# Two-layer S5 and attention trunk: GELU as one ScalarE function, rotation tables kept on chip, tables in buffers of their own, a new order

## The chip, the cores and the metric

One core of one Trainium2 chip runs the whole program. The metric is the device time of one execution in microseconds (us); lower is better. Engines are named as in the profile: PE (TensorE matmul), PEld (its weight loads), DVE (VectorE), ACT (ScalarE), POOL (GpSimd), SP (SyncE, which issues most DMAs).

## The reference

Two layers over 512 tokens of width 1024. Each has an S5 state-space group (32 groups of 16 channels, 64 complex states) and four heads of differential attention on the same modulated input, one output projection, and a SwiGLU channel mixer. Cut to the part that the change touches:

```python
for l in range(DEPTH):                       # 2
    h = x * (1.0 + scale1) + shift1
    u, q, k, v = split(h @ w_in[l])
    # S5: x_t = Lb * x_(t-1) + Bb u_t, complex and diagonal; Lb = exp((a_re + i a_im) * delta)
    y = Re(C x) + d_skip * u
    y = jax.nn.gelu(y)                       # the tanh form: 0.5 y (1 + tanh(sqrt(2/pi) (y + 0.044715 y^3)))
    y = y * sigmoid(y @ glu_w + glu_b)
    att = diff_attention(rot(q), rot(k), v)  # two softmax maps per head, causal
    x = layer_norm(ALPHA * x + (1 + gate1) * (concat(y, att) @ w_out))
    x = layer_norm(ALPHA * x + (1 + gate2) * swiglu(x * (1 + scale2) + shift2))
```

## The kernel before, in words

Every matrix product is made of three single-pass products (high by high, high by low, low by high; `mm3`, L118). A weight tile `wraw` comes by DMA, ACT makes its high part `whi` (`cp`, L113) and DVE, or POOL for a few, the low part `wlo` (L104).

**Layer 0 starts** with a loop over the eight 128-row slices of the input (`START`, L20): for each slice DVE makes two modulation columns (`mraw`, L110), ACT and DVE the two parts of `hT`, PE the products `ups`. In the same loop the S5 parameters are worked out by the generator `s5_params` in five parts; `OPT["par"]` says for each part whether DVE or POOL does it (before: POOL for all but part 2, which holds only ACT's sines). POOL also makes the position angles `rang` there.

**S5 works on four quarters q**, eight groups each. `s5_build` makes the tables of a quarter on DVE (`G`, `QT`, with a temporary `ta`), the short convolution kernel `ksb` that is written to the DRAM array `kd` by DMA and read back by eight DMAs as `M`, and the transposed `Q` (PE `qps`, ACT). `s5_rot` makes cosine and sine of the rotation (`cs`, and `ns` for the negated sine) with ACT's Sin, writes them to the DRAM array `sC` with two DMAs and `s5_gen` reads them back as `csl`. `s5_scan` multiplies (`vps` on PE, then DVE `rp`, `wz`), scans, rotates back and adds the halves with two instructions into the states `S`. `s5_out` makes `yps` on PE and the GELU: ACT Square, a DVE step, ACT Tanh, a second DVE step (both `gl`), ACT Copy into the layout of `y`.

**Two rings of buffers matter.** All S5 work on PE (`kps`, `qps`, `utp`, `vps`, `yps`, `ytps`) shares one PSUM bank (tag "s5", `PB`). The temporaries `ta`, `btmp`, `thl`, `dt`, `ksb`, `cs`, `ns` and `gl` share two buffers (tag "t5", `TB`).

**The order** of the mixer is written in ticks: each short piece of the main products is a tick, and `PLAN[l]` lists for each kind ("s5", "att", "bld", "cs", "mod", "pf") the ticks at which its next step is issued; a scheduler then orders each engine. Layer 1 has the same steps, its tables are built during layer 0's channel mixer and kept in DRAM (`kd`, `sG`, `sQ`, `sC`).

Of the kernel before, what the change touches and what calls it, by code (L numbers as in the profile page):

```python
# [13 lines left out]
AF = mybir.ActivationFunctionType  # L14
# [5 lines left out]
START = ['', '', '', 'v', 'ppvV', 'rpV', 'ApvvA', 'VAVVb']  # L20
LAG, LAG1 = 2, 1
PLAN = ({'bld': [1.264, 2.8128, 2.8128, 7.5302, 15.0069, 15.7908, 16.6324, 22.2347, 24.025, 24.025, 24.025, 31.5693, 31.8037, 32.6247, 36.6694, 39.8654, 39.8664, 44.4181, 55.2875, 55.2875], 's5': [2.4963, 13.7411167, 15.82, 17.6903, 17.9768, 17.9768, 28.1555, 32.3101, 33.8664, 33.8664, 41.8348, 41.8348, 41.8348, 44.9401, 56.3771, 61.9808, 63.9276, 74.4357, 74.4357, 74.9633], 'att': [32.6299, 32.6299, 32.6299, 34.4688, 34.4688, 37.9126, 37.9126, 37.9126, 38.4369, 42.2702, 48.2563, 48.2563, 48.2563, 48.2563, 53.3008, 55.2114, 55.2114, 55.2114, 62.4974, 64.6963, 65.1666, 65.1666, 66.8965, 69.8788, 69.8788, 69.8788, 69.8788, 69.8788, 72.9166, 73.1266492, 78.0578164, 79.4594, 84.4816, 84.4816, 84.4816, 84.4816, 84.4816, 85.7045, 86.611, 86.611, 86.611, 87.1372, 87.1372, 87.1372, 87.1372, 87.1372, 87.1372, 87.1372, 87.1372, 87.1372, 87.7613, 88.3711, 92.1141, 94.0138, 95.5657, 99.9], 'mod': [10.9986, 18.0979, 25.5229, 28.8809, 38.8480964, 39.702, 45.7126, 48.3167, 48.3167, 49.5891, 50.7771, 51.8893, 59.3159, 62.6235, 62.6235, 62.6235, 65.1638, 68.4286, 78.3464, 89.495], 'pf': [15.904, 15.9839, 26.2995, 26.2995, 39.217, 46.2033, 61.5805, 61.9828, 61.9828, 77.3237, 84.6088, 88.9481, 89.2859, 89.9011], 'cs': [2.3738, 2.3738, 3.9308, 15.3106]}, {'s5': [0, 9.5668, 14.1521, 22.5905, 23.0853, 23.0853, 28.7962, 33.7987, 53.4804, 53.9093, 54.6366, 54.6366, 54.6366, 54.89, 57.9461, 62.766, 63.1181, 64.2437, 76.6993, 79.0981], 'att': [32.001, 32.001001, 32.001001, 32.001001, 32.001001, 36.2691, 36.9654, 49.5504, 49.5634, 49.946, 52.2004, 52.2014, 52.2014, 53.123, 53.4199, 53.4634231, 53.4644231, 54.3593, 56.3216, 58.3250688, 61.5574297, 61.5584297, 62.6277, 62.6277, 64.4714996, 64.4715006, 64.4715016, 64.4715026, 64.4715036, 64.4715046, 64.4715056, 64.4715066, 64.4715076, 64.4715086, 64.4715096, 64.4715106, 64.4715116, 64.4715126, 82.7565, 82.7565, 82.7566, 82.7566, 83.9079, 87.4356, 87.4366, 87.4376, 90.018, 91.9921, 91.9931, 91.9941, 91.9951, 91.9951, 91.9951, 91.9951, 91.9951, 99.9], 'pf': [1.9638689, 9.1450603, 14.6524633, 14.6534633, 19.9457, 32.098, 37.9847, 48.098, 51.1731991, 74.7986995, 74.7986995, 81.1276, 84.5849, 86.8909]})
OPT = {'par': [0, 0, 1, 0, 0], 'MODQ': 'sync', 'q_bld': 1, 'q_s5': 0, 'q_att': 0, 'q_pf': 0, 'CSQ': 'scalar', 'plo': [[1, 0, 1, 0, 0, 0, 0, 0, 0, 0, 0, 1, 0, 0, 0, 0, 0, 0], [0, 0, 0, 0, 0, 0, 0, 1, 1, 0, 0, 0, 0, 1, 0, 0, 0, 0]]}
# [3 lines left out]
P = 128  # L27
# [28 lines left out]
T1, T2 = _split_const(2.0 * math.pi, (17,))  # L56
PI_LO = float(np.nextafter(np.float32(math.pi), np.float32(0)))
GELU_C = float(np.float32(math.sqrt(0.044715)))
GELU_S = float(np.float32(math.sqrt(2.0 / math.pi)))
FREQS = [float(np.float32(THETA) ** np.float32(-(2 * i) / ROT)) for i in range(ROT // 2)]  # L60


# [1324 lines left out]
```

## Time and profile before

| | |
|---|---|
| median of 3 runs | 1258.78 us (1256.43 to 1260.86) |
| the profiled execution's own time | 1254.48 us |
| its span, first to last instruction | 1252.7 us |
| mean granted clock of TensorE | 0.985 |
| busy: PE, DVE, ACT, POOL | 1186.2, 813.6, 481.9, 162.3 us |

The span has seven stages: the start of layer 0 (0 to 62 us), its mixer (62 to 286), its channel mixer (286 to 640), the change of layers (640 to 670), and for layer 1 mixer (670 to 881), channel mixer (881 to 1240) and end. A busy time of PE counts a matmul's whole stay in the array, so that a full PE shows 100%. "L107" is a line of the kernel, often that of a helper, so that groups are told apart by tile names.

### The profile page before, as it was taken

Reading aid. Unit: us, or ns where it says so; the run is one execution under the profiler, and the core shown is the slowest. Engines: PE = TensorE matmul, PEld = TensorE weight load, DVE = VectorE, ACT = ScalarE, POOL = GpSimd, SP = SyncE. Lnnn points to the kernel's source line nnn. Section 1 sums busy time; section 2 is a strip of 40 time slices with the busy share of each in tenths; the row PEclk is TensorE's granted clock in tenths of the full one; section 3 lists DMA queues with packets and bytes.
Section 4 is the critical chain, followed back from the end, with each engine's and each line's share of the span. In section 5 each row is a group of like instructions: output and inputs, shape, how many; then the busy total and the mean of one; then the engine's idle time right before and its main releaser. Section 6 shows DMA issues by size and latency. Waiting matters only on the chain.

```text
span 1252.7 us, 17629 instructions
## 1 busy us (share of the span) xinstructions
PE 1186.2 (95%) x6736; PEld 988.7 (79%) x6736; DVE 813.6 (65%) x1505; ACT 481.9 (38%) x848; POOL 162.3 (13%) x289
## 2 busy tenths in 40 slices
PE   4898788999999999999999999999999999999997
PEld 3687676779888888888877788877988888888885
DVE  6779798786787675798558366757665222244556
ACT  3436255536222222343446355553623222234330
POOL 8921230010000010000001243000000000000001
PEclk9899789999999999999999999999999999999999
DMA  9784535535577577645334663223463333333241
GB/s 351 270 209 125 105 84 167 176 128 166 187 256 270 178 234 192 199 157 166 102 98 144 195 178 102 72 97 102 158 192 97 93 100 101 97 89 117 68 134 68
DMA packets 60469, 188.68 MB, mean 151 GB/s; under 512 B 8065, under 2 KB 13985, under 8 KB 60385
## 3 DMA queue, kind: packets, MB, share of 16 engines
q1 hardware_dynamic: 51408, 170.94, 43.0%
q0 software_dynamic: 5088, 13.42, 4.1%
q10 hardware_dynamic: 3888, 3.20, 1.0%
q8 instruction: 53, 0.87, 0.3%
q14 instruction: 32, 0.25, 0.1%
HBM read 172.90 MB, written 12.53 MB: 148 GB/s over the span
## 4 chain that ended last, share of the span: by engine, by line
PE 73%; DVE 11%; POOL 6%; DMA 4%; issue 4%; ACT 2%; DVEq 0%; POOLq 0%; ACTq 0%
PE gps L116 39%; PE dps L116 18%; PE ops L116 4%; PE qkps L116 2%; PE vps L116 2%; POOL s5tmp L104 1%; PE ups L116 1%; DVE wlo L104 1%; DMA wraw<-in_wst 1%; PE glups L116 1%; PE po L116 1%; DVE mraw L110 1%; DVE x L107 1%; PE sps L757 1%; DMA kd<-ksb 1%
## 5 line engine op out<-in xcount | busy, mean ns | idle before, releaser
L104 DVE TENSOR_TENSOR wlo<-wraw,whi 128x1024 fp32r<-128x1024 f32 x180 | 219.6, 1222 | 262.8 <-ACT whi L113 262.1
L113 ACT ACTIVATE whi<-wraw 128x1024 fp32r<-128x1024 f32 x184 | 194.2, 1057 | 390.3 <-PE gps L116 249.8
L116 PE MATMUL gps<-hT2h,whi 128*128 128x512 f32 (+1 forms) x768 | 286.5, 373 | 0.6 <-DVE rtmp L104 0.4
L116 PE MATMUL gps<-hT2l,whi 128*128 128x512 f32 (+1 forms) x768 | 285.8, 372 | 0.0
L116 PE MATMUL gps<-hT2h,wlo 128*128 128x512 f32 (+1 forms) x768 | 285.4, 372 | 0.0
L116 PE MATMUL dps<-whi,ah 128*128 128x512 f32 x704 | 219.6, 391 | 0.0
L116 PEld LDWEIGHTS gps<-hT2h,whi 128*128 128x128 f32 x768 | 144.7, 188 | 26.0 <-DVE rtmp L104 0.9
L116 PEld LDWEIGHTS gps<-hT2l,whi 128*128 128x128 f32 x768 | 144.7, 188 | 24.9
L116 PEld LDWEIGHTS gps<-hT2h,wlo 128*128 128x128 f32 x768 | 144.7, 188 | 24.9
L116 PEld LDWEIGHTS dps<-whi,ah 128*128 128x128 f32 x704 | 132.2, 188 | 28.6 <-DVE rtmp L104 1.2
L116 PE MATMUL dps<-wlo,ah 128*128 128x512 f32 x352 | 137.1, 390 | 0.0
L110 DVE SCALAR_TENSOR_TENSOR mraw<-mraw,scb 128x1024 f32<-128x1024 f32 x96 | 114.2, 1219 | 5.4 <-DMA mraw<-in_modw 5.4
L113 ACT ACTIVATE ah<-aT 128x512 fp32r<-128x512 f32 x88 | 53.6, 626 | 91.2 <-PE dps L116 72.8
L104 DVE TENSOR_TENSOR ah<-aT,ah 128x512 fp32r<-128x512 f32 x88 | 59.3, 688 | 41.3 <-ACT ah L113 41.1
L116 PEld LDWEIGHTS dps<-wlo,ah 128*128 128x128 f32 x352 | 66.1, 188 | 13.4
L116 PE MATMUL ops<-whi,am 128*128 128x512 f32 x128 | 43.1, 398 | 0.0
L761 ACT ACTIVATE e<-sps,nm 128x128 f32<-128x128 f32 (+3 forms) x64 | 33.3, 525 | 19.3 <-DVE nm L759 18.7
L554 POOL DMA_DIRECT2D M<-kd x64 | 33.8, 535 | 41.0 <-DMA kd<-ksb 37.9
L116 PE MATMUL qkps<-wlo,hTh 128*128 128x256 f32 x128 | 38.1, 298 | 0.5 <-DVE wlo L104 0.5
L116 PE MATMUL qkps<-whi,hTh 128*128 128x256 f32 x128 | 37.9, 298 | 0.0
L116 PE MATMUL qkps<-whi,hTl 128*128 128x256 f32 x128 | 37.9, 297 | 0.0
L116 PE MATMUL qkps<-whi,hTnh 128*128 128x256 f32 x128 | 37.4, 293 | 0.0
(285 smaller groups left out, 1858.9 us busy)
## 6 DMA issues: line engine op xcount, KB each, us to landing
wraw<-in_wst SPq DMA_DIRECT2D x184, 512.0 KB, 3.7
mraw<-in_modw SPq DMA_DIRECT2D x96, 512.0 KB, 5.1
M<-kd POOLq DMA_DIRECT2D x64, 64.0 KB, 4.4
gb<-in_lnr SPq DMA_DIRECT2D x8, 512.0 KB, 3.9
csl<-sC SPq DMA_DIRECT2D x8, 384.0 KB, 3.7
xT<-in_xT SPq DMA_DIRECT2D x8, 256.0 KB, 6.7
x<-in_x SPq DMA_DIRECT2D x4, 512.0 KB, 4.6
G<-gd SPq DMA_DIRECT2D x4, 512.0 KB, 4.8
```

The costliest lines, as they stand in the source:

```text
L104: (eng or nc.vector).tensor_tensor(out, a, b, op=op)
L107: nc.vector.scalar_tensor_tensor(out, a, s, b, op0=op0, op1=op1)
L110: nc.vector.scalar_tensor_tensor(out, a, s, b, op0=ALU.mult, op1=ALU.mult, accum_out=acc_out)
L113: nc.scalar.activation(out, in_, AF.Copy, scale=scale)
L116: nc.tensor.matmul(ps, a, b, start=start, stop=stop)
L554: nc.gpsimd.dma_start(M[16 * j : 16 * j + 16], ksrc)
L757: nc.tensor.matmul(ps[:, m, c_], qT[rows, i * P : (i + 1) * P], kT[rows, c_], start=False, stop=c_.stop == n)
L761: nc.scalar.activation(e[:, m, :n], ps[:, m, :n], AF.Exp, bias=nm[:, m : m + 1], accum_out=ss[:, i, m : m + 1])
```

## The change

The GELU of `s5_out` becomes one ACT function that reads PSUM and writes `y`'s layout. In layer 0 `s5_rot` leaves its table in SBUF (`tri`, one buffer of its own) instead of writing it to `sC` and reading it back; it runs for quarter q+1 behind the scan of quarter q. Layer 1 writes its table with one DMA instead of two. `ksb` gets a buffer of its own. The two adds of the states become one instruction. `START`, `PLAN` and `OPT` are new: parts 1 and 3 of the parameters go to DVE, builds are no longer held behind the engine's newest instruction (`q_bld`). Rows of `PLAN` are left out.

```diff
-START = ['', '', '', 'v', 'ppvV', 'rpV', 'ApvvA', 'VAVVb']
+START = ['', 'v', '', 'p', 'vpr', 'VVp', 'vpvA', 'AVbVVA']
...
-OPT = {'par': [0, 0, 1, 0, 0], 'MODQ': 'sync', 'q_bld': 1, 'q_s5': 0, 'q_att': 0, 'q_pf': 0, 'CSQ': 'scalar', 'plo': [[1, 0, 1, 0, 0, 0, 0, 0, 0, 0, 0, 1, 0, 0, 0, 0, 0, 0], [0, 0, 0, 0, 0, 0, 0, 1, 1, 0, 0, 0, 0, 1, 0, 0, 0, 0]]}
+OPT = {'par': [0, 1, 0, 1, 0], 'MODQ': 'sync', 'q_bld': 0, 'q_s5': 0, 'q_att': 0, 'q_pf': 0, 'CSQ': 'scalar', 'plo': [[1, 0, 1, 0, 0, 0, 0, 0, 0, 0, 0, 1, 0, 0, 0, 0, 0, 0], [0, 0, 0, 0, 0, 0, 0, 1, 1, 0, 0, 0, 0, 1, 0, 0, 0, 0]]}
...
-            ksb = t5([P, P], name="ksb")
+            ksb = sm([P, P], "ksb", 1)
...
-            cs = t5([P, 2, 4, 64], name="cs")
+
+            tri = sm([P, 768], "tri", 1)
+            cs = tri[:, 256:].rearrange("p (r g k) -> p r g k", r=2, g=4)
...
-            ns = t5([P, 256], name="ns")
-            ts(ns, flat(st), -1.0, ALU.mult)
-            eng = getattr(nc, "gpsimd" if l else OPT["CSQ"])
-            eng.dma_start(sC[q][:, 256:768], cs.rearrange("p r g k -> p (r g k)"))
-            eng.dma_start(sC[q][:, 0:256], ns)
+            ts(tri[:, 0:256], flat(st), -1.0, ALU.mult)
+            if l:
+                nc.gpsimd.dma_start(sC[q], tri)
+            return tri
...
-            for o in range(2):
-                po, pj = (pr[:, o, j].rearrange("p (g k) -> p g k", g=4)[:, :, 0:63] for j in range(2))
-                tt(S[:, o, :, 1:64], po, pj, ALU.add)
+            po, pj = (pr[:, :, j].rearrange("p o (g k) -> p o g k", g=4)[:, :, :, 0:63] for j in range(2))
+            tt(S[:, :, :, 1:64], po, pj, ALU.add)
...
-            gl = t5([P, 512], name="gl")
-            nc.scalar.activation(gl, ps, AF.Square, scale=GELU_C)
-            stt(gl, gl, 1.0, ps, ALU.add, ALU.mult)
-            nc.scalar.activation(gl, gl, AF.Tanh, scale=GELU_S)
-            stt(gl, gl, 1.0, ps, ALU.add, ALU.mult)
-            cp(yo, gl.rearrange("p (a i c) -> p a i c", a=4, i=8), scale=0.5)
+            nc.scalar.activation(yo, ps.rearrange("p (a i c) -> p a i c", a=4, i=8), AF.Gelu_apprx_tanh)
...
-                C[q] = sm([P, 768], "csl", 1)
-                nc.sync.dma_start(C[q], sC[q])
+                if l:
+                    C[q] = sm([P, 768], "tri", 1)
+                    nc.sync.dma_start(C[q], sC[q])
+
+            def rot(q):
+                C[q] = s5_rot(0, q, pms[0])
...
+            if l == 0:
+
+                seq = [(rot, (0,))] + [(fn, (q + (fn is rot),)) for q in range(4) for fn in (inp, inT, scan, rot, sout)
+                                       if fn is not rot or q < 3]
```

Three places of the new order. **DVE in layer 0's builds**, before: the kernel table `ksb` of quarter 2 and the half `QT` behind it (`ta` is the temporary, `mraw` a modulation column, `gl` the GELU).

```order
L107 SCALAR_TENSOR_TENSOR ksb<-mask_86,s5dt,ksb 128x16
L104 TENSOR_TENSOR QT<-pw,s5bc 128x512
L104 TENSOR_TENSOR ta<-pw,s5bc 128x512
L104 TENSOR_TENSOR QT<-pw,s5bc 128x512
L104 TENSOR_TENSOR QT<-QT,ta 128x512
L104 TENSOR_TENSOR ta<-pw,s5bc 128x512
L110 SCALAR_TENSOR_TENSOR mraw,mods<-mraw,scb 128x1024
L104 TENSOR_TENSOR QT<-QT,ta 128x512
L107 SCALAR_TENSOR_TENSOR gl<-gl,yps 128x512
```
The same engine in the change, at the end of the builds; `rho`, `e`, `nm` are the attention's.

```order
L105 SCALAR_TENSOR_TENSOR e<-e,rho 128x384
L443 COPY s5bc<-s5bc 64x8x16 x2
L102 TENSOR_TENSOR ta<-pw,s5bc 128x512
L102 TENSOR_TENSOR Gt<-pw,s5bc 128x4x128
L102 TENSOR_TENSOR Gt<-Gt,ta 128x4x128
L102 TENSOR_TENSOR ta<-pw,s5bc 128x512
L758 TENSOR_REDUCE nm<-sps 128x2
L102 TENSOR_TENSOR Gt<-Gt,ta 128x4x128
L102 TENSOR_TENSOR QT<-pw,s5bc 128x512 x2
L763 RECIPROCAL rho<-ss 128x1
L105 SCALAR_TENSOR_TENSOR ksb<-mask_86,s5dt,ksb 128x16
```
The builds' `Gt`, `QT` and `ta` now stand among attention steps instead of behind `ksb`, and no `gl` row is left.

**ACT in layer 0's mixer**, before: the GELU of quarter 0 among the attention's work (`e` is the exponential, `wT` the transposed map).

```order
L113 ACTIVATE UU<-u_129 128x512
L634 ACTIVATE gl<-yps 128x512
L113 ACTIVATE wT<-sps 128x384
L636 ACTIVATE gl<-gl 128x512
L785 ACTIVATE e,q_1226<-po 128x128
L113 ACTIVATE wT<-sps 128x512
L113 ACTIVATE y<-gl 128x4x8x16
L113 ACTIVATE UU<-utp 128x512
L785 ACTIVATE e,q_1226<-po 128x128
```
In the change, the GELU of quarter 1 (L629), the rotation's sine and cosine of quarter 2 (`tri`, L224) and the exponentials (L760).

```order
L629 ACT_TABLE_LOAD
L629 ACTIVATE y<-yps 128x4x8x16
L760 ACT_TABLE_LOAD
L760 ACTIVATE e,ss<-sps,nm 128x128 x2
L111 ACTIVATE UU<-utp 128x512
L760 ACTIVATE e,ss<-sps,nm 128x256
L224 ACT_TABLE_LOAD
L224 ACTIVATE tri<-thl 128x256
L225 ACTIVATE tri<-thl 128x256
L111 ACTIVATE wT<-sps 128x128
L760 ACT_TABLE_LOAD
L760 ACTIVATE e,ss<-sps,nm 128x256
```
Three ACT passes have become one, and the three functions bring a table load each time they alternate. Over the whole program the change has 23 table loads where the kernel before has 8: 11 against 3 in layer 0's mixer, 8 against 1 in layer 1's, 4 elsewhere in both.

**POOL in layer 0's mixer**, before: the reads of `M`, and the decay table `dt` and first state `wz` that a scan needs.

```order
L104 TENSOR_TENSOR es<-es,mhalf 128x4
L610 MEMSET wz 128x8
L554 DMA M<-kd_123 16x8x128 x8
L583 COPY dt<-r_396 128x256
L584 MEMSET dt 128x4
L554 DMA M<-kd_123 16x8x128 x2
L610 MEMSET wz 128x8
L554 DMA M<-kd_123 16x8x128 x6
L583 COPY dt<-r_396 128x256
L584 MEMSET dt 128x4
L610 MEMSET wz 128x8
```
The same in the change, for quarters 2 and 3.

```order
L552 DMA M<-kd_123 16x8x128 x8
L581 COPY dt<-r_402 128x256
L102 TENSOR_TENSOR es<-es,mhalf 128x4
L552 DMA M<-kd_123 16x8x128
L582 MEMSET dt 128x4
L552 DMA M<-kd_123 16x8x128
L608 MEMSET wz 128x8
L552 DMA M<-kd_123 16x8x128 x6
L581 COPY dt<-r_402 128x256
```
The second half of the `dt` of quarter 2 now stands behind one read of quarter 3's `M`, which waits for that quarter's `ksb` in DRAM; before it stood ahead. On PE the counts tell the shift: of layer 0's 384 `qkps` matmuls 77 stand behind the last S5 `vps`, before 28, and on DVE 7 of the 16 attention score tiles have had their maximum (`nm`) taken by the last scan's second rotation, before 9.

## Rows read from the trace of the kernel before

**Rows 1.** page: busy us by engine; clock in 40 slices, tenths

```profile
PE 1186.2 (95%) x6736; PEld 988.7 (79%) x6736; DVE 813.6 (65%) x1505; ACT 481.9 (38%) x848; POOL 162.3 (13%) x289
PEclk9899789999999999999999999999999999999999
```

**Rows 2.** windows by stage: PE, PEld, DVE, ACT, POOL busy (count), clock, DMA, GB/s

```profile
0.00:62.00 62.00, 38.63 (x138) 30.13 (x139) 41.57 (x74) 25.60 (x36) 54.89 (x99) 0.92 0.87 311
62.00:205.00 143.00, 119.53 (x1135) 104.75 (x1134) 122.80 (x276) 64.87 (x145) 33.13 (x62) 0.93 0.54 139
205.00:286.00 81.00, 78.12 (x393) 60.79 (x391) 65.56 (x136) 39.06 (x90) 7.39 (x9) 0.98 0.46 146
286.00:640.00 354.00, 353.87 (x1782) 295.72 (x1782) 251.78 (x466) 119.21 (x171) 18.49 (x33) 1.00 0.59 190
670.00:881.00 211.00, 205.02 (x1472) 172.08 (x1471) 135.42 (x271) 103.35 (x230) 39.55 (x72) 1.00 0.41 125
881.00:1240.00 359.00, 358.73 (x1674) 300.40 (x1675) 164.58 (x220) 112.07 (x150) 4.16 (x7) 1.00 0.36 110
```

**Rows 3.** waits of DVE, 60 to 290 us: total us, times, longest us

```profile
DVE ta L104 <- DMA kd<-ksb: 7.1, 1, 7.1
DVE btmp L104 <- POOL pw L104: 4.0, 1, 4.0
DVE thl L104 <- DMA sC<-ns: 1.0, 1, 1.0
```

**Rows 4.** waits of PE, 60 to 290 us

```profile
PE qps L495 <- DVE gl L107: 4.5, 1, 4.5
PE ytps L643 <- DVE gl L107: 1.1, 1, 1.1
```

**Rows 5.** tile gl, 60 to 260 us: ns min/median/max, first, last start

```profile
L107 DVE SCALAR_TENSOR_TENSOR gl<-gl,yps x8: 674/678/690, 125.1 to 201.0; 128x512 f32<-128x512 f32 x8
L634 ACT ACTIVATE gl<-yps x4: 586/597/597, 124.4 to 198.2; 128x512 f32<-128x512 f32 x4
L636 ACT ACTIVATE gl<-gl x4: 628/630/631, 125.8 to 200.4; 128x512 f32<-128x512 f32 x4
L113 ACT ACTIVATE y<-gl x4: 619/630/642, 127.4 to 201.9; 128x512 f32<-128x512 f32 x4
```

**Rows 6.** windows of 4 us behind the longest DVE wait

```profile
156.00:160.00 4.00, 1.02 (x9) 0.81 (x7) 3.59 (x9) 0.52 (x1) 3.06 (x6) 1.00 0.35 52
160.00:164.00 4.00, 2.44 (x12) 2.47 (x13) 3.97 (x12) 3.24 (x9) 1.17 (x3) 0.57 0.78 210
```

**Rows 7.** timeline of ACT, 102.4 to 104 us: start us, us, what

```profile
102.53 1.28 ACT L761 ACT_TABLE_LOAD   x1 [0.76 <-DVE nm L759]
103.82 0.37 ACT L761 ACTIVATE e<-sps,nm 128x128 f32<-128x128 f32 x1
```

**Rows 8.** timeline of ACT, 43 to 44 us

```profile
43.80 0.21 ACT L370 ACTIVATE s5tmp<-s5tmp 128x16 f32<-128x16 f32 x1 [5.04 <-POOL s5tmp L101]
```

**Rows 9.** tile s5tmp: on POOL in layer 0, on DVE in layer 1

```profile
L101 POOL TENSOR_SCALAR s5tmp<-s5tmp x8: 204/292/1057, 25.3 to 45.0; 128x32 f32<-128x32 f32 x6, 128x16 f32<-128x16 f32 x2
L101 DVE TENSOR_SCALAR s5tmp<-s5tmp x8: 180/181/282, 335.5 to 357.2; 128x32 f32<-128x32 f32 x6, 128x16 f32<-128x16 f32 x2
```

**Rows 10.** tile wz, 60 to 200 us

```profile
L104 DVE TENSOR_TENSOR wz<-rp x12: 408/417/691, 107.5 to 195.8; 128x252 f32<-128x252 f32 x8, 128x512 f32<-128x512 f32 x4
L104 DVE TENSOR_TENSOR rp<-wz,csl x4: 1214/1220/1225, 120.3 to 194.2; 128x1024 f32<-128x1024 f32 x4
```

**Rows 11.** window 62 to 270 us, attention score tiles sps alone

```profile
62.00:270.00 208.00, 27.58 (x184) 14.48 (x152) 13.03 (x16) 25.17 (x80) 0.94 0.53 144
```

**Rows 12.** window of 4 us in which PE runs qkps alone

```profile
80.00:84.00 4.00, 4.00 (x36) 4.00 (x34) 2.17 (x5) 1.40 (x3) 0.00 (x0) 1.00 0.77 185
```

**Rows 13.** tile ksb, 60 to 200 us: its DMA to kd

```profile
DMA to landing us min/median/max: 1.6/2.7/9.5
```

**Rows 14.** window 700 to 840 us in three pieces, their sum

```profile
sum 140.00, PE 135.29 PEld 115.01 DVE 91.26 ACT 77.39 POOL 31.27; mean PE 45.10 PEld 38.34 DVE 30.42 ACT 25.80 POOL 10.42
```

More of the change, by code (lines that the diff above doesn't have):

```diff
@@ L57 @@
 PI_LO = float(np.nextafter(np.float32(math.pi), np.float32(0)))
-GELU_C = float(np.float32(math.sqrt(0.044715)))
-GELU_S = float(np.float32(math.sqrt(2.0 / math.pi)))
 FREQS = [float(np.float32(THETA) ** np.float32(-(2 * i) / ROT)) for i in range(ROT // 2)]
@@ L969, in trunk_kernel @@
                 cols += [(0, j) for j in range(16, 40)]
-                rots = list(range(4))
                 def first_x(k):
@@ L1009, in trunk_kernel @@
                                 first_v()
-                            elif c_ == "c":
-                                s5_rot(0, rots.pop(0), pms[0])
                             elif c_ == "p":
@@ L1067, in tick @@
                             prefetch(wb + pfs.pop(0))
-                    elif kind == "cs":
-                        with queued(marks() if OPT["q_bld"] else m0, (POOL,)):
-                            if rots:
-                                s5_rot(0, rots.pop(0), pms[0])
                     elif kind == "bld":
```

2 lines of the change are left out of this document (1 added, 1 removed).

## The prediction, made before the change was run

> **What bounds the kernel now.** I read the busy times first: PE is busy for 95% of the span, no other engine for more than 65%, and the clock row is full but for the second, fifth and sixth of its 40 slices [rows 1]. So time can only come out of stretches where PE is not fed or runs at the lower clock. The windows by stage say where these are [rows 2]. In both channel mixers PE is busy for all but 0.4 us in over 350 (353.87 of 354, 358.73 of 359) at a clock of 1.00: nothing there can move. Layer 1's mixer leaves PE 6 us of 211 idle. Layer 0 is different: its start leaves 23.4 us of 62 idle, the stretch from 62 to 205 us leaves 23.5 of 143, at mean clocks of 0.92 and 0.93, and from 205 to 286 us only 2.9 are idle. In the stretch from 62 to 205 DVE is busy for 122.8 us of 143, ACT for 65 and POOL for 33. So there DVE sets the pace, and PE stalls on what DVE makes late.
>
> The waits of DVE in that stretch name what the change takes up [rows 3]: 7.1 us in one piece, in which a table temporary `ta` waits until the DMA that writes `ksb` to DRAM has landed, since both take their buffer from the tag "t5"; 4.0 us at the start of the first table, for POOL's last parameter; 1.0 us for the write of `sC`. The waits of PE show the same hold-up one step on: `qps` waits 4.5 us and `ytps` 1.1 us until the GELU's second DVE step has read the one S5 bank of PSUM [rows 4]. [...]
>
> **The change, part by part.** First the path of DVE up to the last S5 scan, whose second rotation starts at 194.2 us [rows 10].
>
> 1. `ksb` in its own buffer: the 7.1 us go. What waits for that DMA next is ACT's copy into the one `ksb` buffer of the next quarter, at least a table build later. Ends: 7.1 us gained or, if the wait turns up elsewhere, nothing. I take -7.1.
>
> 2. GELU in one function: in layer 0 eight DVE steps of 0.68 us go, -5.4 us [rows 5]. The PE waits of 4.5 and 1.1 us end with them, but the longer lies behind the same stall as term 1, so I count no more for them.
>
> 3. The table stays on chip: -1.0 us of DVE's wait. The two DMAs per quarter on ACT's queue and the read on SP's cost the other engines nothing that I can see late.
>
> 4. The parameters: 17 small operations leave POOL, where one takes 0.2 to 1.06 us, and join DVE, where the same takes 0.18 us [rows 9]: +3.1 us of DVE work, in the start, where DVE is busy for 41.57 us of 62 [rows 2]. ACT's wait of 5.04 us for the sines' angle, which holds up its work on the next input slices, should go [rows 8], and DVE's 4.0 us for POOL shrink [rows 3]. DVE's new parts stand in its fixed order, so an `hT` slice queues behind them, and part 3 waits for POOL's power. Ends: -4.0 (all of POOL's wait, the cost hidden) and +3.1 us (nothing won). I take -3.0, nearer the first, since the start has DVE time to spare.
>
> 5. States in one step: per quarter two instructions of 0.41 us become one, which the row of the 512-wide form bounds at 0.69 [rows 10]; between 0 and -0.5 us, I take -0.3.
>
> 6. Table loads: the order has 11 in layer 0's mixer instead of 3, 8 more at 1.28 us [rows 7], 10.3 us of ACT. ACT's passes for the GELU shrink from 0.60 + 0.63 + 0.63 us to one, which I take as long as Tanh's 0.63 [rows 5]: 4.9 us less. ACT is idle for more than half of this stretch, so most of the loads hide; but each stands ahead of an exponential or a sine that DVE's next step needs. Ends: 0 and +10.3. I take +4.0, three of eight.
>
> Sum to the last scan: -7.1 - 5.4 - 1.0 - 3.0 - 0.3 + 4.0 = **-12.8 us**.
>
> 7. Given back by the order: in the order of PE 77 of the 384 `qkps` matmuls stand behind the last S5 `vps`, before 28; 49 at 4 us for 36 [rows 12] are 5.4 us. DVE has made 7 attention score tiles by that scan instead of 9; two at 27.58/16 = 1.7 us of PE [rows 11] are 3.4. So 8.8 us of PE work stands behind the scan that stood ahead of it, filling holes. The 2.9 us that PE idles from 205 to 286 take some. Ends: 0 and 8.8, I take 8.8 - 2.9 = +5.9, near the upper, as that stretch has no other room.
>
> Layer 0 thus gives -6.9 us. In layer 1's mixer the same edits meet a full PE: of 140 us around S5 and attention 4.7 are idle [rows 14], which bounds the gain; 7 more table loads at 1.28 us, 9.0 us, bound the loss. I take -1.0. Layer 1's tables are built under a channel mixer in which PE does not wait; one DMA less per quarter costs nothing there, and without that cover its landing (2.7 us at the median for `ksb`'s like write [rows 13]) would show.
>
> Total **-7.9 us**. The profiled execution took 1254.5 us and would take 1246.6. The median of the runs shown is 4.3 us above it, so the forecast for a median is 1258.8 - 7.9 = **1250.9 us**.
>
> [...] The row shows what a change of function set costs here: the load takes 1.28 us and the exponential starts 0.01 us behind its end [rows 7]. [...]
>
> **The rivals.** *More arrives.* If all loads hide and PE has the moved work done before the last scan, as DVE's idle 20 us of 143 [rows 2] leave it room, layer 0 gives -12.8 - 4.0 = -16.8 us and layer 1 -2: 1240 us. Against it: DVE stays the busiest, and PE's work is only moved.
>
> *The wait comes back elsewhere.* In the new order of POOL half of quarter 2's `dt` stands behind a read of quarter 3's `M`, and that waits until quarter 3's `ksb` has landed, 1.6 to 9.5 us after its issue [rows 13]. DVE's scan of quarter 2 waits for `dt`, and all later DVE work behind it. At the upper end, or with another holder of "t5" (`thl` until ACT's sine has read it), term 1's 7.1 us return: -7.9 + 7.1 = -0.8 us, 1258 us, no change. For it: the 9.5 us landing is in the trace. Against: the median is 2.7, and some DVE work stands between that `ksb` and the scan.
>
> *Slower: the table loads set the path.* Around the GELU of quarter 1 ACT's new order has four loads within a dozen instructions, 5.1 us, and attention's exponentials, which PE's transposes and DVE's scalings wait for, stand behind them. In layer 1 PE has no slack to hide it. With all 15 extra loads on the path term 6 is 10.3 instead of 4.0, and layer 1 loses 9.0 instead of gaining 1.0: -7.9 + 6.3 + 10.0 = +8.4, 1267 us. It decides from the point where, beyond the three that I count, six more loads reach the path (6 x 1.28 = 7.7); from there on the change is not faster. For it: function changes fall where the chain is longest. Against: ACT's idle time. [...]
>
> **How the numbers follow.** A measurement of this kernel tells about 0.3%, 3.8 us, from no change. The forecast, between 4 and 14 us faster, has a chance of 0.48; more arriving 0.19; the wait elsewhere, within 3.8 us, 0.18; slower 0.15. So faster 0.67, same 0.18, slower 0.15. The range runs from 1236, below the larger gain by what the lower ends of terms 4 and 5 (1.2 us) and of layer 1 (2.7) still hold, to 1261, a little over no change; outside lie most of the slower case and a few hundredths of the larger gain.
>
> **What would show it.** Right: no DVE wait of `ta` on `kd`; no `gl`; PE's `qps` no longer waiting for a GELU; ACT's wait before the first sine well under 5 us; the last second rotation around 181 us; the channel mixers as long as before. Term 6 shows in DVE's waits for ACT's exponentials, term 7 in how full PE is from that scan to the mixer's end. Wrong: a DVE wait of several us on POOL's `dt` or on ACT, PE at the lower clock in new places, or a layer-1 mixer longer than 211 us.

## The result, and the profile after

The change took **1235.9 us** (median of 4 runs, 1234.9 to 1237.8) against 1257.6 us for the kernel before on the same chip: a ratio of **0.9825, 95% interval 0.9801 to 0.9848**, 21.7 us faster. The forecast was 1250.9 us, with a range from 1236.0. The profiled execution took 1236.3 us with a span of 1234.5; against the span of before (1252.7) that is 18.2 us less. The other 3.5 us of the difference of the medians lie in the execution that was profiled before, which was under its median.

The page after: busy time by engine and the clock row answer to [rows 1].

```profile
PE 1183.6 (96%) x6736; PEld 986.3 (80%) x6736; DVE 805.1 (65%) x1498; ACT 490.8 (40%) x847; POOL 163.2 (13%) x268
PEclk8999899999999999999999999999999999999999
```

PE's busy time has hardly moved (1186.2 before), so what went is idle time. The windows by stage, cut after at the last second rotation of layer 0's S5 (170.6 us) and at the start of its channel mixer (267.6), then as in [rows 2]; the columns are those of [rows 2]:

```profile
0.00:62.00 62.00, 42.95 (x157) 34.20 (x158) 48.37 (x105) 26.74 (x38) 51.46 (x88) 0.92 0.88 313
62.00:170.60 108.60, 96.51 (x954) 82.82 (x953) 100.27 (x218) 55.70 (x111) 29.50 (x54) 0.95 0.52 132
170.60:267.60 97.00, 95.59 (x553) 75.45 (x553) 77.22 (x166) 51.19 (x119) 8.04 (x10) 1.00 0.44 142
268.00:622.00 354.00, 353.38 (x1778) 295.21 (x1779) 252.37 (x468) 119.60 (x171) 23.41 (x31) 1.00 0.60 189
652.00:863.00 211.00, 203.99 (x1480) 173.51 (x1479) 131.01 (x262) 107.85 (x232) 41.82 (x70) 0.99 0.41 126
```

The same cuts in the kernel before, where these points lie at 194.2 and 285.2 us:

```profile
62.00:194.20 132.20, 111.64 (x1057) 98.16 (x1056) 112.60 (x250) 58.16 (x129) 31.82 (x61) 0.92 0.54 135
194.20:285.20 91.00, 85.32 (x468) 66.99 (x467) 74.96 (x159) 45.00 (x102) 8.70 (x11) 0.98 0.47 150
```

Three things stand there. The last second rotation comes **23.6 us earlier** (194.2 to 170.6). From it to the channel mixer now lie 97.0 us instead of 91.0, with PE busy for 95.6 us instead of 85.3 and idle for 1.4 instead of 5.7: **6.0 us are given back**. So layer 0's mixer ends 17.6 us earlier, and nothing else moves much: the channel mixer is as full as before, and layer 1's mixer, from its first `ups` to its first `gps`, takes 221.1 us instead of 222.1 (and 223.5 when the change was run a second time, so that 1 us can't be told here). Ahead of that last rotation DVE was idle for 40.0 us before ((62 - 41.57) + (132.2 - 112.60)) and is now for 22.0: the gain is idle time of DVE far more than work taken from it.

The waits of DVE from 60 to 290 us, which answer to [rows 3]: the waits for `kd`, POOL's `pw` and `sC` are all gone. Of what is left:

```profile
DVE wlo L102 <- ACT whi L111: 9.9, 6, 4.5
DVE es L105 <- ACT e L784: 3.3, 1, 3.3
DVE mraw L108 <- DMA mraw<-in_modw: 2.4, 4, 1.4
DVE rho L763 <- ACT e L760: 0.9, 2, 0.5
DVE tri L102 <- ACT tri L224: 0.3, 1, 0.3
```

Two of these waits in the kernel before, same window:

```profile
DVE mraw L110 <- DMA mraw<-in_modw: 5.4, 7, 2.7
DVE wlo L104 <- ACT whi L113: 3.6, 4, 2.2
```

DVE's groups up to that rotation, before (0 to 194.2 us; busy us, mean ns, then idle before and its releaser):

```profile
L104 DVE TENSOR_TENSOR wlo<-wraw,whi 128x1024 fp32r<-128x1024 f32 x18 | 21.9, 1223 | 13.1 <-ACT whi L113 13.1
L759 DVE TENSOR_REDUCE nm<-sps 128x2 f32<-128x256 f32 (+3 forms) x9 | 6.9, 768 | 0.1
L107 DVE SCALAR_TENSOR_TENSOR e<-e,rho 128x128 f32<-128x128 f32 (+3 forms) x9 | 4.8, 535 | 0.0
L107 DVE SCALAR_TENSOR_TENSOR gl<-gl,yps 128x512 f32<-128x512 f32 x6 | 4.1, 678 | 0.0
L104 DVE TENSOR_TENSOR btmp<-s5bc,kre 128x128 f32<-128x128 f32 x4 | 1.2, 289 | 4.0 <-POOL pw L104 4.0
```

and after (0 to 170.6 us):

```profile
L102 DVE TENSOR_TENSOR wlo<-wraw,whi 128x1024 fp32r<-128x1024 f32 x17 | 20.8, 1234 | 6.6 <-ACT whi L111 6.6
L758 DVE TENSOR_REDUCE nm<-sps 128x2 f32<-128x256 f32 (+3 forms) x7 | 5.3, 764 | 2.0 <-PE sps L756 2.0
L105 DVE SCALAR_TENSOR_TENSOR e<-e,rho 128x128 f32<-128x128 f32 (+3 forms) x6 | 3.0, 501 | 0.0
L102 DVE TENSOR_TENSOR thl<-kio,phihi 128x256 f32<-128x256 f32 x4 | 1.7, 430 | 2.3 <-POOL kim L102 2.3
```

The wait that shrank most ahead of the rotation, beside the 7.1 us for `kd`, is one that the forecast did not have: DVE's low part `wlo` of a weight unit waited 13.1 us for ACT's high part and now waits 6.6. It has not gone from the kernel. In the first 62 us it falls from 9.8 us to 4.4, but from 60 to 290 us it rises from 3.6 to 9.9, and 7.7 of these now stand behind the rotation, where PE is full. And two score tiles fewer stand ahead: `nm` and `e` take 8.3 us instead of 11.7. Only six of the eight GELU steps stood there (4.1 us, not 5.4).

### The profile page after: what moved, and what is told of

Same layout as the page of the kernel before. It is cut to its first block, busy times and chain, and to the rows that moved or that the text cites. A ratio compares the mean times of both kernels' runs of the same rounds, so it can differ in the third digit from the quotient of the medians.

```text
span 1234.5 us, 17541 instructions
## 1 busy us (share of the span) xinstructions
PE 1183.6 (96%) x6736; PEld 986.3 (80%) x6736; DVE 805.1 (65%) x1498; ACT 490.8 (40%) x847; POOL 163.2 (13%) x268
## 5 line engine op out<-in xcount | busy, mean ns | idle before, releaser
L114 PE MATMUL dps<-whi,ah 128*128 128x512 f32 x704 | 219.7, 391 | 0.0
L114 PEld LDWEIGHTS dps<-whi,ah 128*128 128x128 f32 x704 | 132.2, 188 | 28.6 <-DVE rtmp L102 1.2
L760 ACT ACTIVATE e<-sps,nm 128x128 f32<-128x128 f32 (+3 forms) x64 | 33.2, 524 | 13.5 <-DVE nm L758 11.9
L758 DVE TENSOR_REDUCE nm<-sps 128x2 f32<-128x256 f32 (+3 forms) x32 | 26.2, 819 | 17.8 <-PE sps L756 17.7
```

The lines of the kernel that those rows point to most:

```text
L114: nc.tensor.matmul(ps, a, b, start=start, stop=stop)
L758: nc.vector.tensor_reduce(nm, ps[:, :, :n], axis=AX.X, op=ALU.max, negate=True)
L760: nc.scalar.activation(e[:, m, :n], ps[:, m, :n], AF.Exp, bias=nm[:, m : m + 1], accum_out=ss[:, i, m : m + 1])
```

## The experiments

Two kinds. In the first, a part is put back or taken alone and **the scheduler lays each engine's order anew**. Since even a small edit then moves hundreds of instructions, a second kind **holds the order**: each instruction gets a dependency of issue alone, without a semaphore, on the one before it in a list taken from the other kernel.

```
    for v in order:
        for i in regions[-1 - v] if v < 0 else [outside[v]]:
            e = str(i.engine)
            if e in last:
                tc.add_manual_dep(i, last[e].name, NOSYNC, reason="order")
            last[e] = i
```

Here `outside` are the instructions that both kernels have, and `regions` those that an edit put in. Written for the change itself this gives the change's own order, and the time is the same (`change_again`). All ratios are to the kernel before on the same chip in the same round of runs, where its median lay between 1257.3 and 1259.4 us; a difference between two rows of the table is known to some 2 to 4 us (`tanh_held` is 2.1 us over the change by the medians and 4.5 by the ratios). "Rotation" is the start of the last second rotation of layer 0, "mixer" that of its channel mixer, in us of the profiled execution.

| run | us | ratio, 95% | rotation | mixer |
|---|---|---|---|---|
| before | 1257.6 | 1 | 194.2 | 285.2 |
| the change | 1235.9 | 0.9825 (0.9801-0.9848) | 170.6 | 267.6 |
| change_again | 1234.4 | 0.9808 (0.9780-0.9836) | 169.9 | 267.5 |
| oldcode_neworder | 1265.5 | 1.0072 (1.0057-1.0087) | 207.9 | 299.1 |
| newcode_oldorder | 1254.6 | 0.9983 (0.9968-0.9997) | 180.6 | 285.2 |
| before_threeedits | 1258.7 | 1.0006 (0.9985-1.0026) | 185.7 | 284.4 |
| after_oldgelu | 1243.5 | 0.9898 (0.9881-0.9915) | 177.8 | 276.9 |
| after_ksbt5 | 1245.1 | 0.9909 (0.9893-0.9925) | 174.5 | 278.4 |
| after_par_old | 1245.6 | 0.9894 (0.9874-0.9913) | 176.2 | 276.3 |
| after_tanh | 1248.0 | 0.9915 (0.9898-0.9932) | 167.6 | 275.8 |
| after_oldstart | 1242.5 | 0.9874 (0.9853-0.9895) | 168.6 | 274.3 |
| tanh_held | 1238.0 | 0.9861 (0.9838-0.9883) | 170.1 | 267.5 |
| par_held | 1237.7 | 0.9852 (0.9831-0.9873) | 172.9 | 269.9 |
| dve_steps_held | 1241.8 | 0.9887 (0.9865-0.9909) | 172.7 | 270.7 |
| ksb_order | 1240.1 | 0.9870 (0.9849-0.9892) | 169.8 | 273.1 |
| ksb_only_held | 1255.4 | 0.9988 (0.9971-1.0006) | 192.6 | 283.8 |
| threeedits_held | 1271.3 | 1.0118 (1.0097-1.0139) | 195.3 | 288.0 |
| threeedits_first | 1255.7 | 1.0006 (0.9984-1.0028) | 192.0 | 283.8 |
| pool_split_held | 1233.6 | 0.9812 (0.9790-0.9834) | 168.4 | 265.5 |
| all_splits_dve | 1233.0 | 0.9789 (0.9764-0.9814) | 170.9 | 268.3 |

The rotation alone does not rank the runs. `after_tanh` and `after_oldstart` have it at 167.6 and 168.6 us, ahead of the change, and are slower: by then PE has been busy for 129.5 and 130.5 us, in the change for 139.5, and what it has not done stands behind.

### Order without edits, edits without order

`oldcode_neworder`: the kernel before with the three tables of the change (the rotation builds stand in the list "cs" at the times that they have in the change's "s5").

```diff
-START = ['', '', '', 'v', 'ppvV', 'rpV', 'ApvvA', 'VAVVb']
+START = ['', 'v', '', 'p', 'vpr', 'VVp', 'vpvA', 'AVbVVA']
...
-OPT = {'par': [0, 0, 1, 0, 0], 'MODQ': 'sync', 'q_bld': 1, ...
+OPT = {'par': [0, 1, 0, 1, 0], 'MODQ': 'sync', 'q_bld': 0, ...
```

> The kernel before with the change's order alone (start list, plan of both layers, the placement options, the parameters on DVE among them); the rotation tables still go through DRAM, GELU is five steps, ksb shares its buffer. Theory A, the edits carry the gain and the order only moves work: within 4 us of the kernel before, and the 7 us wait of ta for kd is still there. Theory B, the order carries it, by filling the idle start of DVE and PE: 8 to 12 us faster than before, with DVE busy for about 48 us of the first 62, as in the change. Theory C, order and edits need each other: 5 us or more slower than before, since a table read through DRAM now comes too late.

It is 0.7% slower. The waits that the edits take away are back, and PE waits more than before. Some waits of DVE (20 to 290 us), then of PE (60 to 290):

```profile
DVE ta L104 <- DMA kd<-ksb: 6.8, 2, 5.1
PE ytps L643 <- DVE gl L107: 3.4, 1, 3.4
PE utp L575 <- DVE gl L107: 2.8, 3, 1.7
```

`newcode_oldorder`: the change with `START`, `PLAN` and `OPT` of before, the reverse of that diff.

> The change's code with the order of the kernel before (start list, plan, placement options; parameters on POOL again). The four rotation builds, which now have one buffer, stand at the first quarter's input and behind each scan. Theory A, the edits carry the gain: 14 to 18 us faster than before. Theory B, the order carries it: at most 8 us faster. Theory C: within 3 us of before. The wait of ta for kd is gone in all three; in the forecast's terms 1, 2, 3, 5 and 6 it would be 9.8 us faster with nothing given back by the order.

Only 0.2% faster. The rotation comes 13.6 us earlier, close to the forecast's 12.8, and layer 0 ends at 285.2 us as before: all of it is given back. The order alone loses about 8 us, the code alone wins about 2, together they win 22. Neither A nor B holds; C is nearest, but the waits do not bear out its reason, a table in DRAM that comes too late: in `oldcode_neworder` DVE waits 1.9 us for `sC` and 6.8 for `kd`.

The two runs also settle whose the shorter `wlo` wait of the first 62 us is: 4.7 us with the old code in the new order, 9.8 with the new code in the old order, as in the change (4.4) and before (9.8). It belongs to the order tables. The start list and the parameters on DVE each bring a part of it: 7.7 us in `after_oldstart`, 6.3 in `par_held` below.

`before_threeedits`: `ksb` in its own buffer, one-function GELU, states in one step, put into the kernel before.

```diff
-            ksb = t5([P, P], name="ksb")
+            ksb = sm([P, P], "ksb", 1)
...
-            gl = t5([P, 512], name="gl")
...
-            cp(yo, gl.rearrange("p (a i c) -> p a i c", a=4, i=8), scale=0.5)
+            nc.scalar.activation(yo, ps.rearrange("p (a i c) -> p a i c", a=4, i=8), AF.Gelu_apprx_tanh)
...
-                tt(S[:, o, :, 1:64], po, pj, ALU.add)
+            tt(S[:, :, :, 1:64], po, pj, ALU.add)
```

> The kernel before with its order untouched (rotation tables through DRAM, parameters on GpSimd) and three edits: ksb in its own buffer, GELU as one function, states in one step. By the forecast's terms 1, 2, 5 and 6 (-7.1 - 5.4 - 0.3 + 4.0) it is 8.8 us faster than before. Theory that an edit is worth its time only in an order laid for it: between 4 us faster and no change, as with the whole of the change's code in the old order (2.1 us faster), and the last scan stands earlier but the mixer does not end earlier.

No change, as the second theory said.

### Parts put back, order laid anew

`after_oldgelu` (the five GELU steps), `after_ksbt5`, `after_par_old` and `after_oldstart`:

```diff
-            ksb = sm([P, P], "ksb", 1)
+            ksb = t5([P, P], name="ksb")
...
-OPT = {'par': [0, 1, 0, 1, 0], ...
+OPT = {'par': [0, 0, 1, 0, 0], ...
...
-START = ['', 'v', '', 'p', 'vpr', 'VVp', 'vpvA', 'AVbVVA']
+START = ['', '', '', 'v', 'ppvV', 'rpV', 'ApvvA', 'VAVVb']
```

> The change with the GELU of before (Square, two DVE steps, Tanh, copy) in place of the one function, everything else as in the change. By the forecast's terms 2 and 6 (5.4 us of DVE saved, 4.0 lost to table loads) it is 1.4 us slower than the change, 1.0 to 2.4 with layer 1's 1.0. If the table loads hide altogether, 5 to 8 us slower; if the PE waits for the GELU come back too (4.5 and 1.1 us), up to 11. If the table loads cost more than the GELU steps, it is faster than the change.

> The change with ksb back in the tag t5, everything else as in the change. By the forecast's term 1 the wait of a table temporary for the DMA is back: about 7 us slower than the change, with a DVE wait on kd of several us. Rival: in the new order tables and DMA writes are further apart, so the wait is short and hidden: within 3 us of the change, and term 1 was the order's and not the buffer's.

> The change with the S5 parameters of layer 0 on GpSimd as before (17 small operations back from DVE), order and all else as in the change. By the forecast's term 4 it is 3 us slower than the change, between 4 slower and 3 faster. Rival, that the new start has laid the first table so early that it needs the parameters: 6 to 10 us slower, with a DVE wait of several us for GpSimd in the first 70 us.

> The change with the start list of the kernel before: the second half of the weights, the parameters, the rope tables and the first table's build are taken up later among the first 32 products of each of eight steps. Theory that the new start fills holes of PE and DVE in the first 62 us: 4 us slower than the change, the 4.3 us by which PE is less idle there. Theory that this is given back later: within 1.5 us. Theory that the first quarter's chain depends on it: 6 us or more slower, with the first scan about as much later.

By the medians each is slower than the change, by 6.6 to 9.7 us. Read alone, these would give every part its own large share; their sum, 33 us, is more than the change gained. The next run shows why they can't be read so.

`after_tanh` puts Tanh in the place of the GELU, so that it computes another function. It takes table loads away from the change and is slower still:

```diff
-            nc.scalar.activation(yo, ps.rearrange(...), AF.Gelu_apprx_tanh)
+            nc.scalar.activation(yo, ps.rearrange(...), AF.Tanh)
```

> The change with Tanh in the place of the GELU function, one pass of ScalarE as before, but of a function that shares its table with the exponential: S5's output goes through a hyperbolic tangent, so another function is computed, and 5 to 8 of the table loads of layer 0's mixer and all of layer 1's for GELU go. By the forecast's term 6, 4.0 us of the loads are on the path in layer 0: it is 4 us faster than the change, up to 8 with layer 1's. If the loads hide in time in which ScalarE waits anyway: within 1.5 us of the change.

12.1 us slower than the change, with 11 table loads fewer (12 in the program, 23 in the change). Both theories fail.

### The same with the order held

`tanh_held` has the edit of `after_tanh` and the change's order on every engine.

> The change with Tanh for GELU (another function is computed), and each engine's order of instructions held word for word as the change has it, so that only the table loads of ACT differ. In the run without this the scheduler laid a new order and the kernel came out 11 us slower than the change. Theory that the loads are partly on the path (forecast's term 6): 4 to 8 us faster than the change. Theory that they hide: within 1.5 us of the change. Theory that the loss of 11 us came from Tanh itself: about 11 us slower again; if it came from the new order, that loss is gone.

1238.0 us: by the medians the loss is gone but for 2 to 4 us, and no gain is in its place. Windows of layer 0 without (`after_tanh`) and then with the order held, columns as above:

```profile
62.00:170.00 108.00, 90.12 (x907) 78.20 (x906) 98.27 (x213) 51.11 (x101) 28.79 (x54) 0.94 0.50 128
170.00:267.50 97.50, 93.56 (x559) 75.50 (x559) 71.66 (x154) 43.77 (x110) 5.78 (x9) 0.98 0.42 134
```

```profile
62.00:170.00 108.00, 96.75 (x953) 83.47 (x952) 100.37 (x218) 52.97 (x108) 30.27 (x54) 0.94 0.51 132
170.00:267.50 97.50, 95.84 (x555) 75.44 (x553) 77.38 (x166) 48.83 (x117) 8.04 (x10) 1.00 0.44 141
```

Same work, and from 62 to 170 us PE gets 6.6 us less of it done in the one order than in the other. The medians differ by 10.0 us, the profiled executions by 6.6, and layer 0's channel mixers start 8.3 us apart. So **7 to 10 us of the time hang on the order alone**.

In layer 0's mixer the loads that go are not on the path: `tanh_held` has 7 where the change has 11, and rotation and mixer are where the change has them. The other four extra loads, to the sine and back, stay in this run; for them only the small waits of DVE for `rho` and `tri` speak (0.9 and 0.3 us, first section). For layer 1, with 1 load where the change has 8, the run decides nothing. Its mixer takes 219.7 us, against 221.1 in the change and 223.5 in `change_again`. And the profiled execution loses time ahead of it to something that is no table load: a weight unit comes late by DMA, `Q` stands behind it in ACT's queue, and PE waits.

```profile
569.01 1.06 ACT L112 ACTIVATE whi<-wraw 128x1024 fp32r<-128x1024 f32 x1 [8.77 <-DMA wraw<-in_wst]
570.61 0.66 PE L494 MATMUL qps<-ident,QT 128*128 128x128 f32 x4 [4.14 <-ACT Q L112]
```

The trace of the change shows three kinds of load on ACT (start, us, what, idle before):

```profile
96.43 1.28 ACT L629 ACT_TABLE_LOAD   x1
97.72 0.60 ACT L629 ACTIVATE y<-yps 128x512 f32<-128x512 f32 x1
149.97 0.69 ACT L805 ACTIVATE am<-po,gain 128x512 fp32r<-128x512 f32 x1
150.67 1.28 ACT L629 ACT_TABLE_LOAD   x1
153.30 0.60 ACT L629 ACTIVATE y<-yps 128x512 f32<-128x512 f32 x1 [1.34 <-PE yps L626]
181.45 1.28 ACT L760 ACT_TABLE_LOAD   x1 [0.38 <-DVE nm L758]
```

The load at 150.67 us runs as soon as ACT's instruction before it is done, and the GELU behind it then still waits 1.34 us for its matmuls: this load hides. So does one other of the eleven (at 153.91 us, with 1.20 us of wait behind it). Behind the other nine the function starts at once, as at 97.72 us, so that ACT is later by the load. And the load at 181.45 us itself waits for DVE, as the one in [rows 7] does.

`par_held`: the diff of `OPT` above, order held.

> The change with layer 0's S5 parameters on GpSimd as before and every engine's order held as the change has it; the 17 small operations go from DVE's queue into GpSimd's at the place they had in the whole program. Without the order held it was 8.7 us slower than the change. By the forecast's term 4: 3 us slower (between 4 slower and 3 faster). If it is the later parameters that cost, and not the order laid anew: 8 us slower again, with a DVE wait for GpSimd of some 6 us before the first table.

By the medians it is 1.8 to 3.3 us slower than the two measurements of the change, which the intervals can't tell from nothing; rotation and mixer come 2 to 3 us later. ACT waits 5.3 us for GpSimd ahead of the first sine, like [rows 8], and PE's waits of `ups` for `hTh` in the first 62 us rise from 13.3 in the change to 16.1:

```profile
ACT s5tmp L369 <- POOL s5tmp L100: 5.3, 1, 5.3
PE ups L115 <- ACT hTh L112: 16.1, 2, 13.2
```

`dve_steps_held` puts two DVE steps of the old size ahead of each GELU. They work in the PSUM bank itself:

```diff
+            for _ in range(2):
+                ts(ps, ps, 1.0, ALU.mult)
             nc.scalar.activation(yo, ps.rearrange(...), AF.Gelu_apprx_tanh)
```

> The change with two more DVE steps over the 128x512 PSUM bank (times 1) ahead of each GELU, the order held as the change has it: 8 steps in layer 0 and 8 in layer 1, as the old GELU had, and the S5 bank is held longer. By the forecast's term 2 and its view that DVE's time sets the last scan: the last scan of layer 0 some 5.4 us later, and the kernel 5 to 6 us slower than the change (layer 1 hides its own). Rival, that DVE has room to spare in the new order: within 2 us of the change. Rival, that PE waits for the one S5 bank too: 8 us or more slower.

5.9 to 7.4 us slower. The rotation moves 2.1 to 2.8 us, not 5.4, and the channel mixer of layer 0 starts 3.1 us later. Layer 1's mixer, which was not to feel it, takes 224.1 us: 3.0 more than in the change, 0.6 more than in `change_again`, so its share is open. PE now waits for the one S5 bank, which the GELU holds until the steps ahead of it are done (60 to 290 us):

```profile
PE utp L574 <- ACT y L633: 3.9, 3, 1.6
PE ytps L639 <- ACT y L633: 1.1, 1, 1.1
```

In the change PE's wait for the GELU is 0.6 us there. In layer 1's mixer it is 4.6 us here and 0.4 in the change.

`ksb_order`: the change, held in the order that was laid for `after_ksbt5`.

> The change's own instructions and buffers, with every engine's order held as it was laid for the change with ksb back in t5, a kernel that took 1245.1 us. If the 9 us by which that one is slower than the change are the wait for the shared buffer: 1236 to 1238 us here, as the change. If they are the other order: 1243 to 1246 us. Between the two, the parts follow from where it falls.

1240.1 us, between the two: of the 9.2 us by which `after_ksbt5` is slower than the change, 4.2 are its order and 5.0 the shared buffer, as far as the medians tell them apart. The change's own order with the shared buffer was not tried: it needs the buffer.

### The edits in the old order, held

`ksb_only_held`: of the three edits the own buffer for `ksb` alone; every queue as before.

> The kernel before with ksb in its own buffer and nothing else, every engine's order held as before. By the forecast's term 1: 7.1 us faster, with DVE's wait of ta for the DMA gone and the last scan 7 us earlier. Rival, that the freed time is lost behind the next wait in the old order: within 2 us of before.

At most 0.3% faster, and the rotation moves 1.6 us, not 7. The timeline of DVE tells why. Before:

```profile
148.58 0.68 DVE L104 TENSOR_TENSOR QT<-QT,ta 128x512 f32<-128x512 f32 x1
156.41 0.69 DVE L104 TENSOR_TENSOR ta<-pw,s5bc 128x512 f32<-128x512 f32 x1 [7.15 <-DMA kd<-ksb]
157.02 1.22 DVE L110 SCALAR_TENSOR_TENSOR mraw<-mraw,scb 128x1024 f32<-128x1024 f32 x1
```

With its own buffer:

```profile
148.55 0.68 DVE L105 TENSOR_TENSOR QT<-QT,ta 128x512 f32<-128x512 f32 x1
149.15 0.68 DVE L105 TENSOR_TENSOR ta<-pw,s5bc 128x512 f32<-128x512 f32 x1
154.96 1.22 DVE L111 SCALAR_TENSOR_TENSOR mraw<-mraw,scb 128x1024 f32<-128x1024 f32 x1 [5.13 <-DMA mraw<-in_modw]
```

The next instruction in DVE's queue is a modulation column whose own load lands 5.1 us later: the 7.15 us wait **covered** a wait of 5.13. The column starts at 154.96 us instead of 157.02, so 2.1 us are won at this place. Both transfers are slow at this time: the write of `ksb` takes 9.50 us from 146.89 in the kernel before, the column's load 9.92 from 145.02 here. What slows them was not tested. In the change all waits for such loads from 60 to 290 us come to 2.4 us, the longest to 1.4.

`threeedits_held` and `threeedits_first` have all three edits:

> The kernel before with ksb in its own buffer, GELU as one function and states in one step, and every engine's order held as the kernel before has it. Without the order held it was no faster than before (1.0006). By the forecast's terms 1, 2, 5 and 6: 8.8 us faster. Theory that the edits free the time and the order laid anew gave it back: 8 to 14 us faster, with the last scan 10 us or more earlier. Theory that the freed time is worth nothing in the old order: within 4 us of before.

> The kernel before with ksb in its own buffer, GELU as one function at the place in ScalarE's order where Square stood (in the earlier run it stood where the last copy stood, and PE waited 10 us for it in layer 0), and states in one step; the rest of the order as before. By the forecast's terms 1, 2, 5 and 6: 8.8 us faster. Theory that in the old order the freed time is lost: within 4 us of before. If table loads of the exponential's queue cost: slower than ksb_only_held.

In the first the one pass stands where the last copy stood, late in ACT's queue, and holds the only S5 bank: 1.2% slower. The profiled execution has layer 0's channel mixer 2.8 us later than before and a layer-1 mixer of 231.6 us for 222.1. Waits of PE, 50 to 300 us:

```profile
PE qps L496 <- ACT y L636: 4.3, 1, 4.3
PE utp L576 <- ACT y L636: 3.1, 2, 1.7
PE ytps L642 <- ACT y L636: 2.7, 1, 2.7
```

In the second, where `Square` stood, it is no faster than before either. Six DVE steps fewer ahead of the rotation bring it 0.6 us ahead of that of `ksb_only_held`. What DVE saves ahead of the modulation column only lengthens the wait for its load: that wait is now 5.73 us, and the column starts at 155.12 us.

### A cost seen on the way

`pool_split_held` takes one split of a weight unit from GpSimd, `all_splits_dve` all four:

```diff
-'plo': [[1, 0, 1, 0, 0, 0, 0, 0, 0, 0, 0, 1, ...], ...]
+'plo': [[1, 0, 1, 0, 0, 0, 0, 0, 0, 0, 0, 0, ...], ...]
```

> The change with the one split of a weight unit that GpSimd does in layer 0 (the low part of 128x1024, 3.36 us, beside which one DVE instruction of 0.29 us took 2.51) done by DVE at the same place, the order held. If the stretched instruction costs what it seems to: DVE gains 2.2 and pays 1.2, about 1 us faster than the change; else 1 us slower. Within what a measurement tells either way; the trace is to show whether that instruction takes 0.3 us again.

> The change once more, its own order written down instruction by instruction: 1235 to 1237 us, the ground on which the runs with the order held stand. If holding the order itself changed anything, it would show here as more than 2 us of difference to the first runs of the change.

> The change with all four splits of weight units that GpSimd does (one in layer 0, three in layer 1, 2.4 to 3.4 us each) moved to DVE (1.2 us each) at the same places, the order held. If the DVE instructions stretched beside them (2.51 us for 0.29, 2.45 for 0.28) are what they cost: about 2 us faster than the change, 1 us of it in layer 1. If layer 1 has no use for it: as the run with the one split of layer 0 moved, 1233 to 1235 us.

The stretched instruction takes 0.28 us again (last section), but the times, 1233.6 and 1233.0 us, lie 0.8 to 2.9 us under the two measurements of the change and their intervals overlap: a gain is not shown. In the profiled executions layer 0's channel mixer starts at 265.5 and 268.3 us, on either side of the change (267.6 and 267.5). Both are clearly faster than before; that either beats the change is open.

## Why the prediction was wrong

The direction was right, and the likeliest case was too small by more than half. The profiled executions say 18.2 us faster where -7.9 was forecast; by the forecast's own path:

- **Given back (term 7, +5.9): right**, and by its parts: 6.0 us, from 10.3 us more of PE's work behind the rotation (8.8 forecast) less 4.3 us of idle time filled (2.9 forecast).
- **Layer 1 (-1.0): the number agrees**, 222.1 to 221.1 us, but the second run of the change has 223.5. No run shows it.
- **Sum to the last scan (-12.8): the step that failed.** It was -23.6. One term was too high, and one effect was missing.
- **Term 6 (+4.0): too high.** With the order held, 4 loads fewer in layer 0's mixer move neither rotation nor channel mixer, and DVE's waits for ACT's exponentials and sines are 1.2 us in all. "Three of eight" had no row behind it. Only two of the eleven loads hide in a wait behind them; the others make ACT later, and in layer 0 what waited for ACT was not what ended last, as far as these four tell. In the trace of the change each of the eleven takes 1.28 us, and behind the nine that do not hide the function starts 0.01 to 0.02 us after the load's end.
- **What the moved work leaves behind: missing.** Term 7 priced 49 `qkps` and two score tiles behind the scan and let them fill holes ahead of it, at no gain. But 3.4 us of DVE's score work (11.7 to 8.3) went from ahead of the scan, and DVE's idle time there fell by 18.0 us where the terms hold 12.1 (7.1 + 1.0 + 4.0). The largest piece not forecast is `wlo`, 13.1 to 6.6 us: it comes with the order tables, not with the code (4.7 us of it in the start in `oldcode_neworder`, 9.8 in `newcode_oldorder`), and 7.7 us of such waits now stand behind the rotation. What it is worth in time is not shown: `after_oldstart` has more of it in the start and an earlier rotation. Term 6, the score work and `wlo` make 13.9 us where 10.8 are missing; against them stand, among others, one more modulation column (34.6 to 36.5 us) and new waits for `kim` and `sps` (2.3 and 2.0).
- **Term 1 (-7.1): the size by luck.** The wait is gone. But in the old order the buffer is worth 2 us by the medians and 3.7 at the end of the interval (0.29% of 1257.6), as the next instruction was late as well; in an order near the new one it is worth 5.0. The forecast asked what waits for that DMA next, and not what DVE's next instruction waits for.
- **Term 2 (-5.4): too large in layer 0, and by another path.** Six of eight steps (4.1 us) lie ahead of the rotation. Put back with the order held, steps of that size cost 2.1 to 2.8 us at the rotation and 3.1 at the channel mixer; that the whole program loses 5.9 to 7.4 is near the term by luck. And PE's wait for the S5 bank, which the term did not count, is where they show in that run.
- **Term 4 (-3.0): right**, as far as the runs tell: 2 to 3 us at rotation and mixer with the order held, 1.8 to 3.3 by the medians, and by the path it named: ACT's wait before the sine and the input slices behind it. GpSimd's `kim` now makes `thl` wait 2.3 us, which was not forecast.
- **Terms 3 and 5** were not tested alone; the wait for `sC` is gone.

Of the rivals, "more arrives" (1240) is nearest. Its first half, that the loads cost nothing, is shown for the four of layer 0 that `tanh_held` leaves out and open for layer 1; its second, that PE has the moved work done before the scan, is not what happened: that work came behind it, as term 7 says. "The wait comes back elsewhere" did not happen in the change, but it is just what happens when the buffer alone is put into the old order, at a place that the rival did not name. "Slower: the table loads" is refuted by the time.

So the gain is neither the edits' alone nor the order's alone. In `ksb_only_held` a wait of 7.15 us on DVE goes and 2.1 us are won, since the next instruction of the queue was not ready. That the old order was laid around such waits, and the new one around their absence, fits the runs but is shown at this one place only. How much of the 22 us falls to the plan, how much to the start list, and what the tables on chip bring by themselves, the runs do not separate, and so the cause of the missing 10.8 us is shown in part and stays open in part.

## What to carry to other kernels

When a wait goes, read the next instructions of that engine's queue and ask for each when its own operands land; the wait may have been a cover for theirs, and what is left may need a new order to be collected. Price work that an order moves on both sides of the point that it crosses. Where a scheduler lays the order, an edit put back is an edit plus another order (here 4 to 10 us): hold the order of every queue before reading a part's price, or take a run that differs in the order alone. Then read it stage by stage, since one late DMA elsewhere can be as large as the part (in `tanh_held` PE waited 4.14 us behind one).

## What was not expected of the hardware

A DVE instruction that takes 0.28 us elsewhere took 2.51 us beside a split of 3.36 us on GpSimd. In the change, DVE, and beside it GpSimd's split of a weight unit:

```profile
152.58 1.34 DVE L108 SCALAR_TENSOR_TENSOR mraw<-mraw,scb 128x1024 f32<-128x1024 f32 x1
153.86 2.51 DVE L99 TENSOR_SCALAR thl<-thl 128x256 f32<-128x256 f32 x1
```

```profile
152.82 3.36 POOL L102 TENSOR_TENSOR wlo<-wraw,whi 128x1024 fp32r<-128x1024 f32 x1
```

The bounding of 256 columns takes 0.28 us elsewhere, here 2.51, and ends at 156.37 us, 0.19 after GpSimd's ends (152.82 + 3.36 = 156.18). In layer 1 a multiply of 128 columns takes 2.45 us for 0.28 and ends 0.14 us behind such a split. GpSimd takes longer too: its two splits beside such an instruction take 3.36 and 3.38 us, and each began while DVE was in a longer operation of 1024 columns; its two others, with DVE idle, take 2.35 and 2.38. Here the column is done at about 153.86 us, and from there to the split's end are 2.32. The kernel before has such a place as well: one `Gt` step of 2.88 us for 0.68 beside a split at 109.25 us, so the stretch did not come with the change. With the split on DVE (`pool_split_held`) the first one is short:

```profile
152.70 0.28 DVE L100 TENSOR_SCALAR thl<-thl 128x256 f32<-128x256 f32 x1
156.41 1.23 DVE L109 SCALAR_TENSOR_TENSOR mraw<-mraw,scb 128x1024 f32<-128x1024 f32 x1 [1.04 <-DMA mraw<-in_modw]
```

Why the two take longer beside each other, no run shows. Whether the stretch costs time is open, as the times above show: 1.04 of the 2.23 us that DVE gains here go into the wait for the next column's load, and DVE now has the split to do.
